# A two-layer hybrid decoder trunk on one core: how densely the adaLN units are strewn among the first mixer's products

## The chip, the core and the metric

The kernel runs on one core of a Trainium2 chip. TensorE (PE in the profile) multiplies matrices, VectorE (DVE), ScalarE (ACT) and GpSimd (POOL) do the rest, and SyncE (SP) starts nearly all DMA transfers from HBM into the on-chip memory. The engines run side by side, each works through its own list of instructions strictly in order, and they wait for one another by semaphores. The metric is the device time of one execution in microseconds, the median over several.

## The reference

A sequence of 256 tokens of width 2048 goes through two layers. Each layer is a token mixer and a SwiGLU block, and each of these four sub-layers is wrapped in a modulation by a condition vector `c` (adaLN) and a layer norm:

```python
def _ada(c, w, b):
    mod = jax.nn.silu(c) @ w + b
    shift, scale, gate = jnp.split(mod, 3, axis=-1)
    return shift[:, None], scale[:, None], gate[:, None]

# one sub-layer
shift, scale, gate = _ada(c, ada_w[layer, s], ada_b[layer, s])
h = x * (1.0 + scale) + shift
y = f(h)                       # a mixer, or SwiGLU
x = _layer_norm(ALPHA * x + (1.0 + gate) * y, ln_g[layer, s], ln_b[layer, s])
```

`c` is one row, so `silu(c) @ w` with `w` of 2048 x 6144 is a matrix times a vector, four times in all. It is little arithmetic on many bytes: 50 MB of f32 weights for each sub-layer.

The first mixer projects `h` with one combined matrix (`proj = h @ w_in`, 2048 x 7472). A part of the columns goes to an mLSTM of eight heads, the other to an RWKV-7 with sixteen heads of 64; the two results are put side by side and multiplied with `w_out`. The second mixer does the same with retention and gated DeltaNet. All is f32.

## The kernel before

**Products.** A product is 256 tokens times a block of 512 columns of a weight matrix. It is made of units of 512 rows of the weight: one unit is one tile of 1 MB (128 x 2048 f32), loaded by SP into one of three buffers called `raw`. ScalarE rounds its two halves to fp32r (`hi`, L703), VectorE subtracts to get the rest (`lo`, L704), and TensorE multiplies (L718, L719, L720: activation high by weight high, high by low, low by high), 24 matmuls of 128 x 512 for a unit. A projection product (`k.product`) has four units.

**adaLN units.** The matrix times vector is done on VectorE. One adaLN unit is 128 of the 6144 outputs of one sub-layer: a tile of 128 x 2048 f32, again 1 MB, is loaded by SP into a buffer of the same three `raw`, multiplied with the broadcast `silu(c)` and summed along its rows in one instruction (L640). A sub-layer has 48 units: 32 for shift and scale, 16 for the gate. There are 192 in all. The first 32 are done before the first mixer, since `h` needs them. The next 48 are strewn among the products of the first mixer: the gate of this mixer (16) and shift and scale of the SwiGLU block behind it (32). The others come in later blocks.

**The rate.** After each unit of a product `fill` adds a rate to a credit and emits as many adaLN units as the credit holds, up to a limit (80 while the first mixer is emitted):

```python
def fill(self, rate):
    ...
    self.ada_credit = getattr(self, "ada_credit", 0.0) + rate
    while self.ada_credit >= 0.999 and self.ada_next < self.ada_limit:
        self.ada(1)
        self.ada_credit -= 1.0
```

**The first mixer** (`mixer_ab`) has twelve such products, 48 units of `w_ab`. Two further blocks of columns and a narrow one have been computed beforehand (`first_products`). RWKV runs in four batches of four heads (`rwkv`): a front (`rwkv_front`, L1163 to L1214), the heads (`rwkv_heads`: small matmuls L1231 and a triangular inverse in `inverses`, whose first part is a chain of shuffles and multiplications on VectorE from L1004 to L1013, then small matmuls L1017 to L1076, then L1249 to L1262) and an output (`rwkv_out`, L1284 to L1307). Products stand between the batches, as the batches need their columns or as work to put aside: one behind the first batch, three behind the second, four behind the third. These are the first eight products. The last four belong to the second half of the mLSTM and are emitted behind the fourth batch (the first half of the mLSTM stands beside that batch). Columns computed early are parked in HBM (`put_by`) and brought back by SP (`fetch`, L1136).

**The order.** What the program emits is not the order in which it runs. At the end of `body` a planner (`Plan`) takes all instructions with their priorities, which go by the place in the program (splits of weights are preferred by some 2000 places), and a cost for each, and lays out for every engine a fixed list by a simulated run. Buffers of one pool are given out in program order: the three `raw` buffers go to weight tiles and adaLN tiles in just the sequence in which the program asks for them, and a buffer is free when the last instruction that reads it is done.

Of the kernel before, what the change touches and what calls it, by code (L numbers as in the profile page):

```python
# [1869 lines left out]
def body(tc, ins, out):  # L1870
    with ExitStack() as stack:
        k = Trunk(tc, ins, out, stack)
        k.setup()
        k.ada_limit = 32
        h, early = k.first_products()
        x = (ins["x"], None)
        k.ada_limit = 80
        side = k.mixer_ab(h, 48.0 / 32, early)
        x, h = k.mix_out(ins["o_ab"], x, 0, side)
        x, h = k.ffn(0, x, h)  # L1880
        k.ada_limit = 176
        k.mixer_cd(h, 32.0 / 44)
        x, h = k.mix_out(ins["o_cd"], x, 2)
        k.ffn(1, x, h)
        plan = Plan(tc, tc.nc, 250)
        plan.prepare(0)
        order, _ = plan.run([x.bass_priority for x in plan.ins])
        plan.impose(order)
# [18 lines left out]
```

## Time and profile before

| | |
|---|---|
| median of three runs | 2782.91 us (2778.63 to 2790.88) |
| the profiled execution | 2782.83 us, span 2780.7 us |
| PE busy | 2639.4 us, 95% of the span |
| DVE busy | 2010.2 us, 72% |
| ACT busy | 1265.2 us, 45% |
| DMA | 681.61 MB, mean 245 GB/s |

The times of the profile count from the start of the span. The products before the first mixer end at about 120 us, the twelve products of the mixer lie between there and about 600 us, its output product and the norm end at about 740 us. An engine's "busy" is the union of its instructions; a wait is the idle time before an instruction, with what released it; PEclk is the share of full clock that TensorE was granted.

### The profile page before, as it was taken

Reading aid. Unit: us, or ns where it says so; the run is one execution under the profiler, and the core shown is the slowest. Engines: PE = TensorE matmul, PEld = TensorE weight load, DVE = VectorE, ACT = ScalarE, POOL = GpSimd, SP = SyncE. Lnnn points to the kernel's source line nnn. Section 1 sums busy time; section 2 is a strip of 40 time slices with the busy share of each in tenths; the row PEclk is TensorE's granted clock in tenths of the full one; section 3 lists DMA queues with packets and bytes.
Section 4 is the critical chain, followed back from the end, with each engine's and each line's share of the span. In section 5 each row is a group of like instructions: output and inputs, shape, how many; then the busy total and the mean of one; then the engine's idle time right before and its main releaser. Section 6 shows DMA issues by size and latency. Waiting matters only on the chain.

```text
span 2780.7 us, 33791 instructions
## 1 busy us (share of the span) xinstructions
PE 2639.4 (95%) x12906; PEld 2157.6 (78%) x12906; DVE 2010.2 (72%) x3153; ACT 1265.2 (45%) x1704; POOL 78.8 (3%) x88
## 2 busy tenths in 40 slices
PE   5598999999999999999999999999999999999997
PEld 3576777788777887788888888878778888888886
DVE  7899877658777567768767898875866646557557
ACT  2364445556634444443446554444454444443442
POOL 0000000110000000000000201100000000000000
PEclk9899999999999999999999999999999999999999
DMA  9988775235578678878866776675657657666554
GB/s 394 364 295 299 261 255 208 91 107 197 199 286 318 226 266 319 317 259 309 324 232 214 257 258 228 250 268 181 232 196 270 244 197 264 220 215 237 199 183 165
DMA packets 109820, 681.61 MB, mean 245 GB/s; under 512 B 12437, under 2 KB 15705, under 8 KB 31577
## 3 DMA queue, kind: packets, MB, share of 16 engines
q1 hardware_dynamic: 108506, 677.36, 67.0%
q8 instruction: 101, 1.65, 0.2%
q10 hardware_dynamic: 1152, 2.10, 0.2%
q14 instruction: 61, 0.50, 0.1%
HBM read 668.89 MB, written 10.52 MB: 244 GB/s over the span
## 4 chain that ended last, share of the span: by engine, by line
PE 63%; DMA 10%; DVE 9%; issue 4%; ACT 3%; POOL 0%; DVEq 0%; ACTq 0%; SPq 0%; POOLq 0%
PE g L720 19%; PE g L719 19%; PE g L718 19%; DMA raw<-ada 3%; DVE lo L704 3%; DMA raw<-gu 3%; DVE raw L640 3%; DMA raw<-w_cd 2%; ACT hi L703 2%; DMA t<-x 1%; PE m L963 1%; DMA t<-lnrow 1%; DMA raw<-w_ab 1%; PE m L1231 0%; PE m L899 0%
## 5 line engine op out<-in xcount | busy, mean ns | idle before, releaser
L704 DVE TENSOR_TENSOR lo<-raw,hi 128x1024 fp32r<-128x1024 f32 (+2 forms) x802 | 971.4, 1217 | 598.5 <-ACT hi L703 594.1
L703 ACT ACTIVATE hi<-raw 128x1024 fp32r<-128x1024 f32 (+2 forms) x802 | 838.1, 1052 | 1143.6 <-PE g L720 855.6
L718 PE MATMUL g<-hi,h 128*128 128x512 f32 (+2 forms) x2312 | 908.4, 394 | 54.8 <-ACT h L782 38.4
L719 PE MATMUL g<-lo,h 128*128 128x512 f32 (+2 forms) x2312 | 909.9, 394 | 10.2 <-DVE lo L704 9.9
L720 PE MATMUL g<-hi,h 128*128 128x512 f32 (+2 forms) x2312 | 906.2, 392 | 0.0
L718 PEld LDWEIGHTS g<-hi,h 128*128 128x128 f32 x2312 | 439.7, 190 | 152.0 <-ACT h L782 41.3
L719 PEld LDWEIGHTS g<-lo,h 128*128 128x128 f32 x2312 | 440.4, 190 | 107.8 <-DVE lo L704 20.6
L720 PEld LDWEIGHTS g<-hi,h 128*128 128x128 f32 x2312 | 440.1, 190 | 86.3 <-issue 1.7
L640 DVE SCALAR_TENSOR_TENSOR raw<-raw,silu_c 128x2048 f32<-128x2048 f32 x176 | 402.6, 2287 | 31.5 <-DMA raw<-ada 22.7
L718 PE MATMUL g<-hi,a 128*128 128x512 f32 x920 | 361.0, 392 | 5.4 <-DVE t L860 5.4
L719 PE MATMUL g<-lo,a 128*128 128x512 f32 x920 | 360.0, 391 | 0.1
L720 PE MATMUL g<-hi,a 128*128 128x512 f32 x920 | 360.0, 391 | 0.0
L718 PEld LDWEIGHTS g<-hi,a 128*128 128x128 f32 x920 | 173.4, 188 | 41.7 <-DVE t L860 5.8
L719 PEld LDWEIGHTS g<-lo,a 128*128 128x128 f32 x920 | 173.5, 189 | 36.4 <-DVE lo L704 0.9
L720 PEld LDWEIGHTS g<-hi,a 128*128 128x128 f32 x920 | 173.4, 189 | 35.7
L1413 DVE SCALAR_TENSOR_TENSOR f<-c,cols_sb,f 128x253 f32<-128x253 f32 (+2 forms) x120 | 56.0, 476 | 4.7 <-ACT f L1410 3.9
L1614 POOL TENSOR_SCALAR s<-cons_sb,log_alpha 128x128 f32<-128x128 f32 x16 | 15.2, 962 | 1017.7 <-DVE log_alpha L1558 882.9
L1084 POOL TENSOR_SCALAR_AFFINE_SELECT a<-a 128x512 f32<-128x512 f32 (+1 forms) x20 | 27.3, 1372 | 323.1 <-ACT a L1233 178.7
L640 DVE SCALAR_TENSOR_TENSOR a<-a,silu_c 128x2048 f32<-128x2048 f32 x16 | 36.3, 2285 | 0.0
L902 ACT ACTIVATE t<-m,affine 128x128 f32<-128x128 f32 x96 | 35.0, 473 | 0.1
L1231 PE MATMUL m<-y 64*128 64x256 f32 x128 | 29.2, 405 | 3.8 <-DVE a L1234 3.7
L966 ACT ACTIVATE a<-m 128x512 fp32r<-128x512 f32 x44 | 26.1, 592 | 13.5 <-PE m L963 12.3
(476 smaller groups left out, 2052.9 us busy)
## 6 DMA issues: line engine op xcount, KB each, us to landing
raw<-ada SPq DMA_DIRECT2D x176, 1024.0 KB, 5.1
raw<-gu SPq DMA_DIRECT2D x176, 1024.0 KB, 4.9
raw<-dn SPq DMA_DIRECT2D x88, 1024.0 KB, 4.8
raw<-w_cd SPq DMA_DIRECT2D x60, 1024.0 KB, 4.8
raw<-w_ab SPq DMA_DIRECT2D x48, 1024.0 KB, 5.1
a<-ada SPq DMA_DIRECT2D x16, 1024.0 KB, 17.0
raw<-o_ab SPq DMA_DIRECT2D x16, 1024.0 KB, 4.8
raw<-o_cd SPq DMA_DIRECT2D x16, 1024.0 KB, 5.4
```

The costliest lines, as they stand in the source:

```text
L640: v.scalar_tensor_tensor(w[:], w[:], 1.0, self.sc[:], ALU.mult, ALU.mult, accum_out=m[:, i:i + 1])
L703: nc.scalar.activation(hi[:, :2 * n], ws, AF.Copy)
L704: nc.vector.tensor_tensor(lo[:, :2 * n], ws, hi[:, :2 * n], ALU.subtract)
L718: mm(o, ah, wh, start=start and k == 0, stop=False)
L719: mm(o, ah, wl, start=False, stop=False)
L720: mm(o, al, wh, start=False, stop=stop and k == 3)
L902: nc.scalar.activation(h32[:, j, :], b[:, P * j:P * j + P], AF.Identity, bias=self.ab[:, sub + 1, 16 + k:17 + k], scale=self.ab[:, sub + 1 ...
L963: nc.tensor.transpose(b[:, P * k:P * k + P], gs[:, t, P * k:P * k + P], self.ident)
L966: nc.scalar.activation(act[:, 0, :, ts], bv, AF.Copy)
L1084: self.nc.gpsimd.affine_select(x, x, pattern=[[0, n] for n in dims] + [[1, P]], compare_op=ALU.is_gt if strict else ALU.is_ge, fill=0.0, b ...
L1231: mm(b[:, T * x:T * x + T], bk[r, c, x, t, :], ar[r, c, t].rearrange("p x s -> p (x s)"), start=True, stop=True)
L1413: v.scalar_tensor_tensor(o[:, d:T], b[:, T * j:T * j + T - d], self.col(wname, 4 * (tile0 + i + j) + 3 - d), o[:, d:T], ALU.mult, ALU.add)
```

## The change

One number in `body`. The rate for the first mixer is 48/48 in place of 48/32: one adaLN unit behind every product unit in place of three behind every two. The 48 adaLN units were all emitted within the first eight products (32 units); now they reach over all twelve (48 units).

```diff
         k.ada_limit = 80
-        side = k.mixer_ab(h, 48.0 / 32, early)
+        side = k.mixer_ab(h, 48.0 / 48, early)
         x, h = k.mix_out(ins["o_ab"], x, 0, side)
```

The number of instructions of each kind stays. Their order moves, and this on all engines, since the planner lays out the lists anew. Three places follow. In the rows the names are those of the program with a running number: `raw` is a buffer of the three, `w_ab` the mixer's weights, `ada` the adaLN weights, `by` a parked block.

SP, at the start of the mixer's first product, before:

```order
L681 DMA raw_1255<-w_ab 128x2048
L681 DMA raw_1289<-ada 128x2048
L681 DMA raw_1292<-ada 128x2048
L1158 DMA q_780<-lw 65x256
L1159 DMA q_780<-la 96x256
L1160 DMA q_780<-lg 128x256
L681 DMA raw_1295<-w_ab 128x2048
L681 DMA raw_1329<-ada 128x2048
L681 DMA raw_1332<-w_ab 128x2048
L681 DMA raw_1366<-ada 128x2048
L681 DMA raw_1369<-ada 128x2048
```

and with the change:

```order
L681 DMA raw_1255<-w_ab 128x2048
L681 DMA raw_1289<-ada 128x2048
L681 DMA raw_1292<-w_ab 128x2048
L1158 DMA q_780<-lw 65x256
L1159 DMA q_780<-la 96x256
L1160 DMA q_780<-lg 128x256
L681 DMA raw_1326<-ada 128x2048
L681 DMA raw_1329<-w_ab 128x2048
L681 DMA raw_1363<-ada 128x2048
L681 DMA raw_1855<-w_ab 128x2048
```

Between two weight tiles stood one adaLN tile and two in turn; now there is one each time.

SP, around the fetch of parked blocks (L1136) that stands between the loads of the tenth and the eleventh product, before:

```order
L681 DMA raw_4569<-w_ab 128x2048
L681 DMA raw_4603<-w_ab 128x2048
L1136 DMA q_3901<-by_3345 128x512 x2
L1136 DMA q_3905<-by_3514 128x4x128 x2
L681 DMA raw_4677<-w_ab 128x2048
L681 DMA raw_4711<-w_ab 128x2048
```

and with the change:

```order
L681 DMA raw_4561<-ada 128x2048
L681 DMA raw_4564<-w_ab 128x2048
L1136 DMA q_3841<-by_3291 128x512 x2
L1136 DMA q_3845<-by_3454 128x4x128 x2
L681 DMA raw_4598<-ada 128x2048
L681 DMA raw_4647<-w_ab 128x2048
L681 DMA raw_4681<-ada 128x2048
L681 DMA raw_4684<-w_ab 128x2048
```

The last sixteen weight tiles had no adaLN tile among them; now each has one.

DVE, in the heads of the third RWKV batch, between the last step of its front and the products with its state (L1255), before:

```order
L1209 TENSOR_TENSOR q_3531<-c_3585,z_3540 128x256
L1061 COPY y_2609<-m_2712 32x8x32
L1061 COPY y_2609<-m_2713 32x8x32
L1185 RECIPROCAL v_3534<-gg_3598 128x1
L1198 SCALAR_TENSOR_TENSOR y_3530<-z_3551,minus_kk,gg_3598 128x2x128
L1186 TENSOR_TENSOR v_3534<-v_3534,gg_3598 128x1
L1199 TENSOR_TENSOR y_3530<-z_3541,gg_3598 128x2x128
L704 TENSOR_TENSOR lo_4538<-raw_4535,hi_4537 128x1024
L1255 TENSOR_TENSOR s_2805<-m_2794,v_2359 128x256
```

and with the change:

```order
L640 SCALAR_TENSOR_TENSOR raw_4411,modulation<-raw_4411,silu_c 128x2048
L1209 TENSOR_TENSOR q_3471<-c_3525,z_3480 128x256
L640 SCALAR_TENSOR_TENSOR raw_4487,modulation<-raw_4487,silu_c 128x2048
L1061 COPY y_2579<-m_2682 32x8x32
L1061 COPY y_2579<-m_2683 32x8x32
L1185 RECIPROCAL v_3474<-gg_3538 128x1
L1198 SCALAR_TENSOR_TENSOR y_3470<-z_3491,minus_kk,gg_3538 128x2x128
L1186 TENSOR_TENSOR v_3474<-v_3474,gg_3538 128x1
L1199 TENSOR_TENSOR y_3470<-z_3481,gg_3538 128x2x128
L704 TENSOR_TENSOR lo_4456<-raw_4453,hi_4455 128x1024
L640 SCALAR_TENSOR_TENSOR raw_4524,modulation<-raw_4524,silu_c 128x2048
L1255 TENSOR_TENSOR s_2775<-m_2764,v_2329 128x256
```

Here no adaLN unit stood; now three do (L640), and a fourth stands right ahead of the second L1255 of this batch.

Counted along DVE's list from one L1004 (the start of a batch's inverse) to the next, the mixer's 48 adaLN units stood 12 ahead of the first batch's, then 19, 15 and 2, and none behind the fourth's. Now they stand 8, 10, 12, 9, and 9 behind the fourth's. The number of weight halves (L704) that precede the fourth batch's L1004 is the same in both lists, 99, and so is the number of product matmuls that precede the third batch's output on PE (L1306), 48.8 units, twelve units of `first_products` among them.

## The prediction

> **What bounds the kernel now.** First the page: who is busy, and whether evenly.
>
> ```profile
> span 2780.7 us, 33791 instructions
> ...
> PE 2639.4 (95%) x12906; PEld 2157.6 (78%) x12906; DVE 2010.2 (72%) x3153; ACT 1265.2 (45%) x1704; POOL 78.8 (3%) x88
> ...
> PE   5598999999999999999999999999999999999997
> ...
> PEclk9899999999999999999999999999999999999999
> DMA  9988775235578678878866776675657657666554
> ```
>
> TensorE sets the pace as a whole. A change that moves work of VectorE and DMA can only give back time in which TensorE waits or runs at a lower clock, or take more of it. So the second view is the busy time by stretches of the first mixer (from about 120 us on).
>
> ```profile
> core 0: us, PE busy (x) PEld busy (x) DVE busy (x) ACT busy (x) POOL busy (x), PEclk, DMA share, GB/s
> ...
> 215.00:260.00 45.00, 35.44 (x140) 26.92 (x139) 40.09 (x86) 13.50 (x15) 0.00 (x0) 0.92 0.90 342
> ...
> 345.00:385.00 40.00, 34.58 (x141) 27.56 (x140) 34.25 (x65) 10.18 (x13) 0.00 (x0) 0.83 0.77 288
> ...
> 470.00:500.00 30.00, 30.00 (x305) 26.15 (x303) 14.62 (x37) 15.46 (x31) 0.00 (x0) 1.00 0.21 72
> 500.00:528.00 28.00, 23.06 (x97) 15.16 (x97) 20.58 (x92) 14.43 (x37) 7.33 (x11) 0.82 0.13 38
> 528.00:600.00 72.00, 71.92 (x530) 62.01 (x529) 45.84 (x132) 38.05 (x65) 4.91 (x10) 1.00 0.34 118
> ```
>
> Two stretches lose: 215 to 260 has 45.00 - 35.44 = 9.56 us of idle PE, and a granted clock of 0.92, which is 0.08 x 35.44 = 2.84 us more; 345 to 385 has 5.42 us idle and 0.17 x 34.58 = 5.88 us of clock. In both VectorE is at 86 to 89% and DMA at 77 to 90%. Beyond 470 us it is the other way round: VectorE and DMA have room, PE is full but for 500 to 528. Third, the waits of PE in 215 to 385, and one of them in order of time:
>
> ```profile
> PE g L718 <- ACT hi L703: 10.7, 6, 3.0
> PE g L719 <- DVE lo L704: 3.2, 6, 0.5
> PE m L1017 <- DVE y L1013: 1.2, 2, 1.0
> ```
>
> ```profile
> 218.55 0.39 PE L720 MATMUL g<-hi,h 128*128 128x512 f32 x1
> 221.72 0.73 PE L718 MATMUL g<-hi,h 128*128 128x512 f32 x2 [2.79 <-ACT hi L703]
> 222.98 0.79 PE L719 MATMUL g<-lo,h 128*128 128x512 f32 x1 [0.53 <-DVE lo L704]
> 223.57 0.63 PE L720 MATMUL g<-hi,h 128*128 128x512 f32 x1
> 224.00 0.63 PE L718 MATMUL g<-hi,h 128*128 128x512 f32 x1
> ...
> 226.81 0.39 PE L718 MATMUL g<-hi,h 128*128 128x512 f32 x1
> 227.04 0.40 PE L719 MATMUL g<-lo,h 128*128 128x512 f32 x1
> ```
>
> Nearly all the waiting is for weights that haven't been split (10.7 + 3.2 us), and behind such a wait matmuls follow at 0.43 us in place of 0.23 for some 3 us: the clock loss belongs to the same stalls. Why the weights are late stands in SP's list:
>
> ```profile
> 213.29 0.33 SPq L681 DMA_DIRECT2D raw<-w_ab  x1
> 216.13 0.33 SPq L681 DMA_DIRECT2D raw<-ada  x1
> 220.13 0.33 SPq L681 DMA_DIRECT2D raw<-w_ab  x1
> 224.19 2.65 SPq L681 DMA_DIRECT2D raw<-ada  x2
> 230.58 0.33 SPq L681 DMA_DIRECT2D raw<-w_ab  x1
> ...
> 261.40 0.33 SPq L681 DMA_DIRECT2D raw<-w_ab  x1
> ```
>
> From 213.29 to 261.40 six weight tiles and nine adaLN tiles pass through the three buffers, 8.02 us for a unit of product. TensorE needs 24 x 0.2275 = 5.46 us for one (0.2275 is the step between matmuls from 226.81 on).
>
> **The change, part by part.** *The supply.* A product unit brings 2 tiles through the buffers in place of 2.5. If a tile keeps its time, a unit comes every 8.02 x 2/2.5 = 6.41 us. The shortfall against 5.46 goes from 2.56 to 0.95 us, so 63% of the loss goes. If the weights that were split ahead, or other work of PE, fill the rest, all goes. The loss is 9.56 + 2.84 + 5.42 + 5.88 = 23.7, less 1.2 us for the wait on L1013, which isn't one for weights: 22.5 us. So 14.2 to 22.5 us come back. Where between them, I take from VectorE's list:
>
> ```profile
> L640 DVE SCALAR_TENSOR_TENSOR raw<-raw,silu_c 128x2048 f32<-128x2048 f32 x50 | 114.2, 2284 | 4.1 <-DMA raw<-ada 4.0
> L704 DVE TENSOR_TENSOR lo<-raw,hi 128x1024 fp32r<-128x1024 f32 x72 | 89.4, 1246 | 32.0 <-ACT hi L703 31.7
> ```
>
> An adaLN unit is 2.284 us of VectorE. Up to the start of the fourth batch's inverse the new list has 39 of them in place of 48 and the same number of halves to split; PE has the same product units behind it when the third batch puts out its result. Nine units fewer are 9 x 2.284 = 20.6 us. VectorE does not pace all of that time, but this lies within the bounds and near the end at which PE is kept full. I take 20.6.
>
> The starts of the four inverses show the same from the side of the batches:
>
> ```profile
> 206.75 0.29 DVE L1004 TENSOR_TENSOR e<-s 128x128 f32<-128x128 f32 x1
> ...
> 322.30 0.28 DVE L1004 TENSOR_TENSOR e<-s 128x128 f32<-128x128 f32 x1
> ...
> 438.34 0.28 DVE L1004 TENSOR_TENSOR e<-s 128x128 f32<-128x128 f32 x1
> ...
> 517.74 0.28 DVE L1004 TENSOR_TENSOR e<-s 128x128 f32<-128x128 f32 x1
> ```
>
> 115.6 us with 19 adaLN units between two starts, 116.0 with 15, and 79.4 with 2.
>
> *Units that come to stand in the third batch's heads.* Four now lie on VectorE between that batch's front and its second L1255, where there was none. There its list is a chain with PE:
>
> ```profile
> 479.38 0.42 DVE L1209 TENSOR_TENSOR q<-c,z 128x256 f32<-128x256 f32 x1 [0.38 <-PE c L1208]
> 482.08 0.88 DVE L1061 COPY y<-m 32x256 f32<-32x256 f32 x2 [2.27 <-PE m L1058]
> ...
> 490.02 1.23 DVE L704 TENSOR_TENSOR lo<-raw,hi 128x1024 fp32r<-128x1024 f32 x1 [5.44 <-ACT hi L703]
> 492.34 0.42 DVE L1255 TENSOR_TENSOR s<-m,v 128x256 f32<-128x256 f32 x1 [1.10 <-PE m L1253]
> ```
>
> Behind the new units wait L1061 and L1255, and behind these the matmuls L1069 and L1261. VectorE sat idle there for 2.27 and 5.44 us, so a unit may fit in free of cost, or an instruction comes while it runs. Bounds: 0 and 4 x 2.284 = 9.1 us. I take half a unit each, 4.6 us, since no row tells at which moment of the wait the unit starts.
>
> *Nine units behind the fourth batch's L1004.* 20.6 us of VectorE and 9 MB of transfers move to where VectorE is busy 45.84 of 72 us, DMA 34% and PE 71.92 of 72: the product matmuls of PE hide them, so 0. If this cover were gone, up to 9 x 2.284 = 20.6 us.
>
> *SP.* Nine issues of 0.33 us move past the fetch of parked blocks, at which the queue stands for long:
>
> ```profile
> SPq L1136 <- PE c L1306: 43.9, 1, 43.9
> ```
>
> The fetch waits for a tile that the third batch's output frees, and this does not change; behind it now stand an adaLN tile and then the weights of the eleventh product, one tile (some 3.2 us, from 48.1 us for 15 tiles) later. PE has products left at that time: 0.
>
> *Elsewhere.* The planner lays out the second mixer a little differently too, with the same instructions. PE is idle for 22.5 us there in all:
>
> ```profile
> sum 700.00, PE 677.52 PEld 562.24 DVE 550.22 ACT 343.19 POOL 41.19; mean PE 24.20 PEld 20.08 DVE 19.65 ACT 12.26 POOL 1.47
> ```
>
> (1400 to 2100 us.) No row says which way this goes: 0, with some 5 us to either side.
>
> **The sum**, against the profiled execution (2782.83 us, 2.1 us more than its span, and within 0.1 us of the median): 2782.83 - 20.6 + 4.6 = 2766.8, say **2767 us**. Own range with the bounds: 2782.83 - 22.5 = 2760 to 2782.83 - 14.2 + 9.1 = 2778.
>
> **The rivals.** *Only traded (2778 us).* The stalls go by the low rule (14.2 us) and the four units in the third batch's heads cost their full 9.1 us: 2782.83 - 14.2 + 9.1 = 2777.7. For it: that batch is where PE is least covered (23.06 of 28 us, clock 0.82) and the batches' spacing above was shortest where the list had only 2 units. Against: at 470 to 500, where the four lie, PE is busy 30.00 of 30.
>
> *The clock does not come back (2775 us).* Behind the second stretch PE ran slowly while it was busy:
>
> ```profile
> 372.00:378.00 6.00, 5.67 (x26) 5.61 (x27) 3.84 (x9) 2.00 (x3) 0.00 (x0) 0.57 0.58 210
> ```
>
> If that goes with the small matmuls of the heads, and not with the stalls, only the idle time returns: 14.98 - 1.2 = 13.8 us, of it 20.6/22.5, 12.6 us; 2782.83 - 12.6 + 4.6 = 2774.8. [...]
>
> *All comes back (2760 us).* 22.5 us, and the four units fit into the idle time of VectorE: 2782.83 - 22.5 = 2760.3.
>
> *Slower (2798 us).* The units land where the batches are chains: all four in the third batch's heads and the nine behind the fourth's start cost their full length, 13 x 2.284 = 29.7 us, against 14.2 us: 2782.83 + 15.5 = 2798.3. It decides from the point where more than six of the thirteen (14.2 / 2.284) are waited for in full. For it: L1061, L1255 and their like in the fourth batch queue right behind units. Against: 71.92 of 72 us of PE at 528 to 600.
>
> **How the numbers follow.** The forecast has a chance of 0.48, only traded 0.20, clock 0.10, all 0.12, slower 0.10. A measurement here tells about 0.5%, 13.9 us, from no change: below 2769.0 is faster, above 2796.8 slower. The forecast lies just beyond the first bound, 0.6 of its chance is faster (0.29), with all 0.12 and 0.05 from the spread of the others: 0.46. Slower: 0.09 of the last. The same: 0.45. For 8 in 10 the range leaves out most of the last rival and reaches past "all" by the 5 us of the second mixer and some noise: 2752 to 2789.
>
> **What would show it.** In the changed kernel's profile, the waits of PE for L703 and L704 between 200 and 385 us should fall from 13.9 to under 4 us, with a clock of 0.97 or more there; the first, second and third gaps between the starts L1004 should be about 95, 109 and 95 us (each by its number of units: -9, -3, +7), the fourth start 20 us or more earlier; PE stays full from there to 600 us. It is wrong if weights still come late at two tiles for a unit, if waits for L1061 or L1255 by several us appear in the third batch, or if PE falls below 95% busy in the 80 us behind the fourth start.

## The result

The changed kernel takes 2769.61 us in the median of 10 runs (2756.61 to 2783.07), the kernel before 2785.36 us in 10 runs beside it (2776.68 to 2790.88): a ratio of 0.9939, 95% interval 0.9918 to 0.996. In a second set it took 2766.66 us (11 runs, 2757.38 to 2786.43) against 2783.28 (20 runs): 0.9934, 0.9912 to 0.9956. So it is faster by 16 us, 0.6%, and the forecast of 2767 us is met. Single runs of either kernel lie further apart than this (the changed one's by 26 to 29 us in a set, those of the kernel before by 14 to 35), so only medians and means over many runs can show it.

### The profile page after: what moved, and what is told of

It is laid out like the page before. It is cut to its first block, busy times and chain, and to the rows that moved or that the text cites. A ratio compares the mean times of both kernels' runs of the same rounds, so it can differ in the third digit from the quotient of the medians.

```text
span 2762.5 us, 33778 instructions
## 1 busy us (share of the span) xinstructions
PE 2633.9 (95%) x12906; PEld 2155.9 (78%) x12906; DVE 2007.0 (73%) x3153; ACT 1263.0 (46%) x1702; POOL 78.7 (3%) x88
## 4 chain that ended last, share of the span: by engine, by line
PE 67%; DMA 15%; DVE 12%; ACT 3%; issue 2%; POOL 0%; SPq 0%; DVEq 0%; ACTq 0%; POOLq 0%
PE g L720 20%; PE g L719 20%; PE g L718 20%; DMA raw<-ada 5%; DMA raw<-gu 4%; DVE lo L704 4%; DVE raw L640 4%; DMA a<-ada 2%; ACT hi L703 2%; DMA raw<-w_cd 1%; PE m L963 1%; DMA raw<-w_ab 1%; DMA y<-w_ab 1%; DMA t<-x 1%; PE m L1231 1%
## 5 line engine op out<-in xcount | busy, mean ns | idle before, releaser
L704 DVE TENSOR_TENSOR lo<-raw,hi 128x1024 fp32r<-128x1024 f32 (+2 forms) x802 | 968.4, 1214 | 581.9 <-ACT hi L703 579.1
L703 ACT ACTIVATE hi<-raw 128x1024 fp32r<-128x1024 f32 (+2 forms) x802 | 837.7, 1052 | 1132.2 <-PE g L720 877.4
L719 PE MATMUL g<-lo,h 128*128 128x512 f32 (+2 forms) x2312 | 909.6, 393 | 10.7 <-DVE lo L704 10.5
L640 DVE SCALAR_TENSOR_TENSOR raw<-raw,silu_c 128x2048 f32<-128x2048 f32 x176 | 402.7, 2288 | 43.7 <-DMA raw<-ada 35.5
L640 DVE SCALAR_TENSOR_TENSOR a<-a,silu_c 128x2048 f32<-128x2048 f32 x16 | 36.3, 2285 | 0.0
L963 PE MATMUL m<-cons_sb,q 128*128 128x128 f32 x176 | 28.4, 285 | 6.1 <-DVE q L960 6.1
L963 PEld LDWEIGHTS m<-cons_sb,q 128*128 128x128 f32 x176 | 21.0, 144 | 13.4 <-DVE q L960 12.0
```

What stands on the lines that cost most here:

```text
L640: v.scalar_tensor_tensor(w[:], w[:], 1.0, self.sc[:], ALU.mult, ALU.mult, accum_out=m[:, i:i + 1])
L703: nc.scalar.activation(hi[:, :2 * n], ws, AF.Copy)
L704: nc.vector.tensor_tensor(lo[:, :2 * n], ws, hi[:, :2 * n], ALU.subtract)
L719: mm(o, ah, wl, start=False, stop=False)
L963: nc.tensor.transpose(b[:, P * k:P * k + P], gs[:, t, P * k:P * k + P], self.ident)
```

## The profile after

The page of the changed kernel, in the order of the prediction:

```profile
span 2762.5 us, 33778 instructions
...
PE 2633.9 (95%) x12906; PEld 2155.9 (78%) x12906; DVE 2007.0 (73%) x3153; ACT 1263.0 (46%) x1702; POOL 78.7 (3%) x88
...
PE   5699999999999999999999999999999999999997
...
PEclk8799999999999999999999999999999999999999
DMA  9966765546588578778866775665657657666554
```

The shares of the whole have hardly moved; the difference is seen only by stretches. The busy time in the stretches that the prediction looked at (times from the start of the span; the batches now start 14 to 29 us earlier, so the last three rows hold other work than before):

```profile
200.00:385.00 185.00, 181.51 (x1161) 145.92 (x1161) 153.37 (x359) 92.34 (x168) 5.78 (x8) 1.00 0.67 247
215.00:260.00 45.00, 43.66 (x337) 35.70 (x337) 39.49 (x74) 21.32 (x33) 0.00 (x0) 1.00 0.82 301
345.00:385.00 40.00, 38.16 (x328) 30.08 (x326) 28.91 (x74) 21.50 (x51) 2.00 (x2) 1.00 0.56 206
470.00:500.00 30.00, 25.18 (x110) 17.39 (x109) 22.94 (x97) 16.91 (x38) 7.36 (x11) 0.89 0.22 71
500.00:528.00 28.00, 28.00 (x153) 24.03 (x152) 27.05 (x59) 15.73 (x25) 0.00 (x0) 1.00 0.69 244
528.00:600.00 72.00, 68.66 (x480) 57.04 (x480) 55.26 (x140) 37.91 (x70) 11.28 (x15) 0.95 0.55 200
```

The same first row of the kernel before:

```profile
200.00:385.00 185.00, 166.31 (x884) 129.89 (x883) 163.05 (x344) 79.46 (x133) 8.63 (x10) 0.94 0.77 280
```

From 200 to 385 us PE is idle for 185 - 181.51 = 3.5 us, where it was idle for 18.7; its clock is 1.00 in place of 0.94, and VectorE does 9.7 us less. The waits of PE in this stretch, all that are left:

```profile
PE m L1231 <- DVE a L1234: 1.0, 3, 0.7
PE g L719 <- DVE lo L704: 0.7, 2, 0.4
PE m L1069 <- ACT y L1062: 0.6, 1, 0.6
PE m L1069 <- DVE y L1061: 0.5, 1, 0.5
PE c L1179 <- DVE z L1094: 0.5, 1, 0.5
```

The wait for `hi` (10.7 us before) is gone and that for `lo` went from 3.2 to 0.7. SP's list shows the tiles in turn, one and one:

```profile
215.56 0.33 SPq L681 DMA_DIRECT2D raw<-ada  x1
218.17 0.33 SPq L681 DMA_DIRECT2D raw<-w_ab  x1
...
251.28 0.33 SPq L681 DMA_DIRECT2D raw<-ada  x1
252.42 0.33 SPq L681 DMA_DIRECT2D raw<-w_ab  x1
258.45 0.33 SPq L681 DMA_DIRECT2D raw<-ada  x1
```

Six product units in 258.45 - 215.56 = 42.89 us, 7.15 us each, where six took 48.11. The step worked out from the tiles alone was 6.41 us. The buffers are not what it waits for now: no weight is late by more than 0.4 us. The four inverses start at

```profile
192.69 0.29 DVE L1004 TENSOR_TENSOR e<-s 128x128 f32<-128x128 f32 x1
288.81 0.28 DVE L1004 TENSOR_TENSOR e<-s 128x128 f32<-128x128 f32 x1
392.31 0.28 DVE L1004 TENSOR_TENSOR e<-s 128x128 f32<-128x128 f32 x1
488.38 0.28 DVE L1004 TENSOR_TENSOR e<-s 128x128 f32<-128x128 f32 x1
```

96.1, 103.5 and 96.1 us apart, against 115.6, 116.0 and 79.4.

## The experiments

The table gives each run that follows: time and ratio to the kernel before, the fourth start of L1004, the issue of the first gate row (L673, behind the fourth batch), and the waits of PE for split weights (`hi` and `lo`) from 120 to 600 us. The last three are of one profiled execution each, which need not be near the median. Line numbers shift by a few where a kernel has lines added.

| kernel | median us | ratio (95%) | fourth start | gate row | waits for weights |
|---|---|---|---|---|---|
| before | 2785.36 | | 517.74 | 637.21 | 14.5 |
| before, again | 2780.81, one run | | 515.79 | 636.06 | 13.3 |
| changed | 2769.61 | 0.9939 (0.9918 to 0.996) | 488.38 | 610.64 | 0.7 |
| changed, again | 2766.66 | 0.9934 (0.9912 to 0.9956) | 503.82 | 626.12 | 0.5 |
| sums cut short | 2770.87 | 0.9949 (0.9931 to 0.9967) | 507.80 | 628.35 | 12.9 |
| loads cut short | 2766.26 | 0.994 (0.9916 to 0.9964) | 500.57 | 620.99 | 9.1 |
| third gap's sums cut | 2762.93 | 0.9919 (0.9892 to 0.9946) | 483.22 | 605.33 | 0.5 |
| last nine sums cut | 2765.39 | 0.993 (0.9902 to 0.9958) | 497.66 | 617.82 | 2.3 |
| six units with five | 2776.79 | 0.9977 (0.995 to 1.0005) | 508.67 | 628.69 | 7.0 |
| eight units with nine | 2783.18 | 0.9986 (0.9956 to 1.0017) | 487.57 | 629.68 | 3.3 |
| changed, extra matmuls | 2770.13 | 0.9928 (0.9897 to 0.996) | 492.40 | 625.19 | 4.7 |
| before, extra matmuls | 2774.96 | 0.9965 (0.9936 to 0.9994) | 502.81 | 627.57 | 18.6 |

Every run, profiled or not, has its span and its mean granted clock. So span x (1 - clock) is counted as what the clock took from it, and the rest of the span as work and idle time. The means over the runs, with those of the kernel before that ran beside them (for the first row its 41 runs of two sets; standard errors: 0.8 to 3.1 us for the clock, 0.7 to 2.6 for the rest):

| kernel | taken by the clock | before | rest of the span | before |
|---|---|---|---|---|
| changed, 21 runs | 57.1 | 59.5 | 2709.1 | 2722.9 |
| sums cut short | 50.9 | 58.9 | 2717.3 | 2723.4 |
| loads cut short | 47.5 | 60.0 | 2717.9 | 2722.4 |
| third gap's sums cut | 54.9 | 60.0 | 2704.9 | 2722.4 |
| last nine sums cut | 53.9 | 60.0 | 2709.7 | 2722.4 |
| six units with five | 64.4 | 60.0 | 2711.6 | 2722.4 |
| eight units with nine | 64.0 | 61.8 | 2717.8 | 2724.6 |
| changed, extra matmuls | 52.4 | 61.8 | 2715.5 | 2724.6 |
| before, extra matmuls | 52.5 | 61.8 | 2723.9 | 2724.6 |

### Both kernels a second time

No edit. What was expected of the kernel before:

> The kernel before once more, for a second execution in profile. The two profiles so far differ by 25.6 us up to the norm behind the first mixer (722.6 and 697.0 us), but the block behind it, in which both programs hold the same instructions in the same order, took 748.4 us in the one and 758.8 in the other. If these 10 us are the spread of executions, this one's SwiGLU block lies anywhere from 745 to 760 us while its fourth inverse start lies within 3 us of 517.7. If they belong to the changed kernel, it lies within 3 us of 748.

and of the changed one:

> The changed kernel once more. Fourth inverse start within 3 us of 488.4, norm within 4 us of 697. If the 10 us in the SwiGLU block are the spread of executions, that block takes anything from 745 to 760 us and the ratio stays near 0.994 only because both kernels' later parts vary; if the changed kernel causes them, it takes 756 to 761 us again.

The two profiles of the kernel before are alike: all four starts within 2 us (206.61, 321.10, 437.31, 515.79), the waits for weights 9.8 + 3.5 us. Those of the changed kernel are not. (This is no property of the new order alone: over 20 to 29 runs the kernel before scatters by 24 to 35 us.) Its waits for weights are gone again (0.5 us), but its starts are 193.76, 297.60, 407.93 and 503.82, 15 us later at the fourth than in the first profile, with the same instructions in the same order. In 200 to 385 us PE is as busy as in the first profile, at a lower clock:

```profile
200.00:385.00 185.00, 181.49 (x1088) 147.52 (x1086) 143.89 (x318) 87.08 (x149) 3.79 (x6) 0.92 0.65 238
```

The head of a batch shows where it is lost. The second execution, from just before the first L1069 (254.02 us) on:

```profile
250.00:254.00 4.00, 4.00 (x109) 2.82 (x107) 3.94 (x6) 3.85 (x6) 0.00 (x0) 1.00 0.42 133
254.00:258.00 4.00, 3.39 (x37) 2.98 (x36) 1.35 (x2) 2.87 (x9) 0.00 (x0) 0.86 0.96 393
258.00:262.00 4.00, 4.00 (x21) 4.00 (x20) 1.28 (x2) 0.53 (x2) 0.00 (x0) 0.50 0.63 221
262.00:266.00 4.00, 4.00 (x14) 3.42 (x15) 2.11 (x7) 1.06 (x1) 0.00 (x0) 0.50 0.33 139
...
270.00:274.00 4.00, 4.00 (x17) 3.63 (x16) 0.48 (x3) 1.24 (x4) 0.00 (x0) 0.50 0.73 254
274.00:278.00 4.00, 4.00 (x30) 3.44 (x30) 0.43 (x1) 1.29 (x4) 0.10 (x1) 1.00 0.02 8
```

and the first execution (L1069 at 253.12 us):

```profile
254.00:258.00 4.00, 3.61 (x40) 3.40 (x40) 1.88 (x1) 2.50 (x8) 0.00 (x0) 1.00 0.97 401
258.00:262.00 4.00, 4.00 (x31) 3.75 (x31) 2.86 (x9) 1.06 (x1) 0.00 (x0) 1.00 0.65 219
262.00:266.00 4.00, 4.00 (x33) 3.66 (x33) 4.00 (x7) 1.23 (x4) 0.00 (x0) 1.00 0.14 59
```

For some 16 us the clock is 0.50 in the one and 1.00 in the other, with PE busy 4.00 us in each row from 258 to 274 us in the one and 3.82 to 4.00 in the other. This one dip made the first gap 103.8 in place of 96.1 us (a gap is the time from one start of L1004 to the next). What PE does as the clock falls:

```profile
254.02 0.67 PE L1069 MATMUL m<-y,a 64*64 64x64 f32 x8
255.30 0.68 PE L1069 MATMUL m<-y,a 64*64 64x64 f32 x8 [0.61 <-ACT y L1062]
255.91 0.43 PE L1249 MATMUL m<-q,a 128*128 128x64 f32 x2
256.27 1.46 PE L1076 MATMUL m<-y,P 64*64 64x64 f32 x16
257.66 1.54 PE L1249 MATMUL m<-q,a 128*128 128x64 f32 x6
```

64-wide matmuls, one wait of 0.61 us, and no product until 262.38 us. Counted over the heads of the first three batches, the clock fell to 0.50 right behind L1069 in 7 of 12 heads of the four profiles with the changed order (the first two, and the two below with sums cut in it), and in none of 12 of the four profiles with the order of before. In these one or several product matmuls stand between the groups in most heads, though one head of before has 5.8 us without any and kept its clock both times. The order of before has its half-clock stretches in other places: from 120 us to the gate row the clock took 20.5 us in both its profiles, 15.4 and 29.0 in the two of the changed kernel.

The SwiGLU block behind the mixer (from the first DMA of L920 at the end of one norm to that of the next) took 748.5 and 753.0 us in the kernel before, 758.9 and 758.8 in the changed one. So a part of the first difference is the spread of executions, and the 6 to 10 us that are left come with the changed kernel.

### The sums of the adaLN units cut short

In the kernel before, order unchanged; the 48 units of the mixer are summed over 256 of their 2048 columns:

```diff
+        n = 256 if 32 <= u < 80 else D
-        v.scalar_tensor_tensor(w[:], w[:], 1.0, self.sc[:], ALU.mult, ALU.mult, accum_out=m[:, i:i + 1])
+        v.scalar_tensor_tensor(w[:, :n], w[:, :n], 1.0, self.sc[:, :n], ALU.mult, ALU.mult, accum_out=m[:, i:i + 1])
```

> Rate 48/32 as before and the order of the kernel before on every engine, all 48 adaLN tiles loaded in full, but the sum of the mixer's 48 units runs over 256 of 2048 columns (7/8 of these sums are left out), so about 0.5 us of VectorE in place of 2.28. If VectorE's time makes the weights late (the term of 20.6 us: so many units, so much VectorE), the waits of PE for the split weights fall from 14.5 to under 4 us, the fourth inverse start comes at 490 us or earlier and the whole time falls by 20 us or more. If the loads through the three buffers do (15 tiles in 48 us, DMA at 90%), at least half of the waits stay, the start lies at 503 us or later and the time falls by under 12 us.

A sum falls from 2.284 us to 0.416:

```profile
L641 DVE SCALAR_TENSOR_TENSOR raw<-raw,silu_c 128x256 f32<-128x256 f32 x48 | 20.0, 416 | 8.8 <-DMA raw<-ada 8.8
```

This takes 48 x 1.87 = 90 us from VectorE, and the fourth start comes 8 to 10 us earlier, the time falls by 12 to 14 us: 8.0 us of it by the clock and 6.1 by the rest. The waits for weights stay at 12.9 us:

```profile
PE g L719 <- ACT hi L704: 8.5, 6, 4.0
PE g L720 <- DVE lo L705: 4.4, 8, 0.8
```

So VectorE's time is a part of what the adaLN units cost, but by itself not what makes the weights late.

### The loads of the adaLN units cut short

In the kernel before, order unchanged; each of the 48 tiles loads 256 of its columns, and VectorE works on seven times these:

```diff
+        elif 32 <= u < 80:
+            w = self.raw_p.tile([P, 2048], F32, tag="raw", name=self.name("raw"))
+            nc.sync.dma_start(w[:, :256], src[:, :256])
...
+            seven = lambda x: x.rearrange("p (r n) -> p r n", r=7)
+            v.scalar_tensor_tensor(seven(w[:, 256:]), w[:, :256].unsqueeze(1).to_broadcast([P, 7, 256]), 1.0, seven(self.sc[:, 256:]), ALU.mult, ALU.mult, accum_out=m[:, i:i + 1])
```

> The kernel before, its order unchanged on every engine; each of the first mixer's 48 adaLN tiles loads only 256 of its 2048 columns, while VectorE's sum keeps nearly its length (seven times the same 256 columns, 1792 in place of 2048). Theory 'loads': the weights are late because nine adaLN tiles of 1 MB pass through the three buffers beside six weight tiles. Then the waits of PE for L703 and L704 in the mixer fall from 14.5 us to under 4, the fourth L1004 starts at 495 us or earlier (before: 517.7 and 515.8), and the time falls by 18 us or more. Theory 'VectorE': the sums hold up the splits. Then the waits stay at 11 us or more, the fourth start at 512 or later, and the time within 8 us of before. With the shortened sums having given about half of the gain, a share of both would show as a fourth start between these.

Between the two: the fourth start at 500.57 us, 16 us earlier, the time 17 us less, the waits for weights 9.1 us in place of 14:

```profile
PE g L727 <- ACT hi L712: 5.1, 5, 1.8
PE g L728 <- DVE lo L713: 4.0, 8, 0.7
```

The sums still take 2.01 us each. The loads are the larger part of the lateness (5 of 14 us of the waits, against 1 us for the sums), and neither alone ends it. Most of the 17 us, though, came by the clock, which took 12.5 us less; the rest of the span fell by 4.5 us, no more than with the sums cut (6.1). Why the clock gained is not shown. The account that fits both: a tile holds its buffer for the load and for the sum, so either keeps the next weight out, and taking the whole unit away, as the change does nine times up to the fourth start, removes both. This is argued, not shown. Load and sum were not cut in one kernel, so it stays open whether a tile's place in the sequence of the three buffers costs something even when both are short. Both theories were too simple.

### Six units with every five

```diff
-        side = k.mixer_ab(h, 48.0 / 32, early)
+        side = k.mixer_ab(h, 48.0 / 40, early)
```

> Five... six adaLN units with every five product units in place of three with every two (48.0 / 40): a middle way. Units up to the four L1004: 41, 54, 66, 78, against 44, 63, 78, 80 before and 40, 50, 62, 71 in the changed kernel. If the supply of weights sets the gain, the first two gaps (13 and 12 units against 19 and 15) get most of it already: waits for L703 and L704 under 5 us and a fourth start of 495 to 508 us, the time 6 to 14 us below before. If only the full step down to one unit matters, waits stay at 9 us or more and the time within 5 us of before.

Waits 7.0 us, half of before; fourth start 508.67; 6.4 us faster, with an interval that reaches just past 1. The waits lie between the two bounds that were set, and the start just misses its own. Beside the clock the gain is 10.8 us, of the 13.8 of the whole change; the clock took 4.4 us more, about twice the error of this difference. So what the units cost beside the clock falls as they are taken out of the early gaps, and the clock hides a part of it.

### The sums of the third gap cut short

In the changed kernel, order unchanged:

```diff
+        n = 256 if 62 <= u < 71 else D
```

with the line of the sums as above.

> The changed kernel, its order unchanged; the nine adaLN units between the third and the fourth L1004 are summed over 256 columns in place of 2048, some 18 us less of VectorE there. If the adaLN units cost what the forecast's sum gives them (2.284 us each of the path), the third gap falls from 96 us to about 80 and the time by some 16 us. If instead TensorE's own products fill that gap now (two product units more than in the kernel before stand in it), the gap stays within 4 us of 96 and the time within 6 us of the changed kernel.

The third gap is 483.22 - 393.65 = 89.6 us, against 96.1 and 95.9: 6.4 us less for 9 x 1.87 = 16.8 us of VectorE. But the clock differs too. The gap here, and in the first profile of the changed kernel:

```profile
393.65:483.22 89.57, 86.88 (x565) 69.21 (x563) 57.44 (x188) 46.44 (x87) 3.69 (x5) 1.00 0.64 231
392.31:488.38 96.07, 91.94 (x565) 72.91 (x563) 73.62 (x189) 46.68 (x87) 3.68 (x5) 0.95 0.59 216
```

The same 565 matmuls keep PE busy for 86.88 us at full clock and for 91.94 at 0.95. The idle time falls only from 4.1 us (5.5 in the second profile) to 2.7: 1.4 to 2.8 us for the 16.8, so a unit costs some 0.1 to 0.2 of its length in this gap. What made the gap grow from 79.4 to 96 us is PE's own work: 565 matmuls where there were 512, 2.2 product units more (2.2 x 5.46 = 12.0 us), and the lower clock. The prediction's "about 95, by its number of units" gave the right size from a rule that does not hold.

### The last nine sums cut short

```diff
+        n = 256 if 71 <= u < 80 else D
```

> The changed kernel, its order unchanged; the last nine adaLN units, behind the fourth L1004, are summed over 256 columns in place of 2048, some 18 us less of VectorE there. The prediction's step: the products of TensorE hide them, they cost 0. Then the stretch from the fourth L1004 to the fetch of the first gate row (L673) stays at 120 us or more (122.3 us in both profiles of the changed kernel, 119.5 in that of the kernel before), and the time within 5 us. If they cost their length (the rival 'slower'), the stretch falls to about 104 us. If part of the cover is missing, to 115 or so.

From the fourth start to the gate row: 617.82 - 497.66 = 120.2 us, against 122.3 in both profiles of the changed kernel. Taking 16.8 us of the nine sums away gains 2 us at most; TensorE hides the rest. The time is within 5 us of the changed kernel.

### Eight units with every nine, the rest behind the gate row

The change carried on, to see where that cover ends:

```diff
-        side = k.mixer_ab(h, 48.0 / 48, early)
+        side = k.mixer_ab(h, 48.0 / 54, early)
...
         self.gate = self.gate_rows(self.a8, sub)
+        if sub == 0:
+            self.ada(max(0, 80 - self.ada_next))
```

> The change carried on: eight adaLN units with every nine product units (48.0 / 54), and the rest, behind the first gate row, at once. Units up to the four L1004: 38, 48, 56, 64 in place of 40, 50, 62, 71, so 16 in place of 9 behind the fourth. By the third gap's experiment (89.6 us with nine sums cut short, 96 with nine full ones) the third gap falls by 0 to 5 us; by that of the last nine (2 us at most) the seven more behind the fourth start cost 0 to 4 us, or 16 us if the cover of TensorE is used up by the nine. So the time is 2 us shorter to 5 us longer than the changed kernel; 10 us longer would say that the cover ended.

The cover ended, which was not expected. The fourth start is at 487.57 us, no earlier than the best of the changed kernel, and from there to the gate row it takes 142.1 us in place of 122.3. This stretch, and the same of the changed kernel:

```profile
487.57:629.68 142.11, 126.97 (x758) 102.42 (x757) 121.31 (x284) 70.75 (x120) 22.11 (x24) 0.95 0.65 237
488.38:610.64 122.26, 116.80 (x715) 96.75 (x716) 101.75 (x263) 72.19 (x121) 17.43 (x24) 0.94 0.56 198
```

Of the 20 us, 9.7 are idle time of PE (15.1 in place of 5.5 us) for seven units more (16.0 us of VectorE); the other 10.2 are 43 matmuls more, work that stood ahead of the fourth start. By the ratios the time is 14 us above that of the changed kernel. Set against the kernel before, each in its own set, 7.0 us of the gain beside the clock are gone, and the clock took 2.2 us more where the changed kernel has 2.4 less. The waits of PE from the fourth start to the gate row:

```profile
PE g L718 <- ACT hi L703: 6.3, 2, 5.3
PE g L719 <- DVE lo L704: 2.6, 2, 2.3
PE c L1305 <- DVE s L1307: 2.0, 2, 1.4
```

and the place, behind the product rows, where the output's weights are late:

```profile
600.00:630.00 30.00, 21.08 (x87) 15.10 (x87) 27.80 (x49) 17.97 (x35) 10.86 (x7) 0.77 0.76 283
```

The wait for `hi` is back, 9 us idle over this row and a clock of 0.77: the same stall as before the change, in another place.

### Extra matmuls in the heads

Is it the stretch without a product that brings the clock down? In the changed kernel, eight matmuls of 128x512 for each of the first three batches, written ahead into banks that the small matmuls then overwrite:

```diff
+    def warm(self, x):
+        for _ in range(2 if self.hot is not None else 0):
+            self.nc.tensor.matmul(x[:], self.hot[:, 0, 0, 0:P], self.hot[:, 0, 0:2, :].rearrange("p k t -> p (k t)"), start=True, stop=True)
...
             x = self.bank()
+            self.warm(x)
             for j in range(4):
                 mm(x[64:, 64 * j:64 * j + 64], mt[:64, hs.start + j, 64:], d[:64, hs.start + j, :64], start=True, stop=True)
...
             xb = self.bank()
+            self.warm(xb)
```

> The changed kernel with 24 matmuls more in the first mixer's heads: ahead of the first writes into four of the small matmuls' banks of each of the first three batches, two matmuls of 128x512 whose result is overwritten (8 x 0.23 = 1.8 us for a batch, 5.5 us in all). Nearly all else keeps its order. In the changed kernel the granted clock fell to 0.50 for 7 to 12 us behind the first L1069 in 7 of 12 heads seen so far, where some 5 us of 64-wide matmuls stand without a product between them. Theory 'gaps between products': the dips come from these stretches. Then no head, or one of three, shows the dip; the clock loss of a run (span x (1 - granted clock), 57.1 us in the mean over 21 runs of the changed kernel) falls by 6 us or more, and the times scatter less than 29 us; the time comes out within 5 us of the changed kernel, since 5.5 us are paid. Theory 'chance': the dips do not depend on what PE does there. Then some half of the heads show it, the clock loss stays at 55 us or more, and the time is some 5 us longer.

and the same in the kernel before:

> The same 24 matmuls in the kernel before, where none of 12 heads seen in this order had the dip. It measures what they cost by themselves: some 5 us slower than before if PE is full there, 0 if they fall into its waits; the clock loss of a run stays near the 59.5 us of the 41 runs of before. If that falls by 6 us too, the extra matmuls act on something else than the heads' dips.

In the changed kernel with the extra matmuls the clock takes 52.4 us in the mean of 12 runs (standard error 3.1), against 57.1 (1.5) in 21 runs without; the rest of the span grows by 6.4 us (2709.1 to 2715.5), about the 5.5 us that the matmuls need. The fall of 4.7 us lies between what the two theories asked for, and its own error is 3.4 us. Of the profile's three heads one has the dip, a long one. The time came out even, and the runs scatter no less (2745.18 to 2789.84). So this run does not decide between the theories.

In the kernel before the loss falls as well, from 61.8 us (standard error 1.9, 29 runs of the same set) to 52.5 (2.8, 10 runs), with no dip in any head in either, and the rest of the span stays (2724.6 and 2723.9): the time falls by 10 us, and all of it is clock. In the profile two half-clock stretches that both profiles of before have, 10.24 us each in 369 to 383 and in 516 to 527 us, are missing. So more went than dips behind L1069. But the extra matmuls are not the only thing that moved: the plan was laid out anew, 46.5 product units in place of 48.8 precede the fourth start on PE, and the waits for weights rose to 18.6 us. So these runs show that the clock's loss can fall by some 10 us from one kernel to another (61.8 to 52.5 us here; 60.0 to 47.5 with the loads cut short, where the order is that of the kernel before); that the extra matmuls themselves hold the clock up they do not show.

## Why the prediction was right, and where it was not

**The supply (-20.6 us).** The mechanism holds. The waits for L703 and L704 fell from 13.9 to 0.7 us (forecast: under 4). The fourth start came 29 us earlier in one profile and 13 in the other, 19 with the last nine sums cut (which can't matter before it): 20 in the mean, with the clock's share in it. From 120 us to that start PE runs the same 2118 matmuls in both orders and is idle for 29.9 and 28.4 us before, 12.2 and 16.1 after: 12 to 18 us less, where the term had 12.6 us of idle time. The size of 20.6 us came from a price that does not hold, VectorE's 9 x 2.284 us, after a section that laid the lateness to the buffers. The two cuts show load and sum both at work, and the third gap shows a unit at 0.1 to 0.2 of its length where weights aren't late. That it is the stalls that make a unit dear fits this, but no run shows it by itself.

**What of it was clock.** Of the 22.5 us, 8.7 were clock, laid to the stalls. (The rows give somewhat more, 0.08 x 45.00 + 0.17 x 40.00 = 10.4 us: the clock is a mean over the whole stretch, so it goes with its length and not with PE's busy time.) The clock of those stretches did come back in the first profile: 1.00 in 215 to 260 and in 345 to 385. In the second it was 0.92 from 200 to 385, where the forecast asked for 0.97. Over the runs, the clock's share is 57.1 us (21 runs of the changed kernel) against 59.5 (41 runs of the kernel before): 2.4 us came back, within the error of 1.9. The step that failed is "the clock loss belongs to the same stalls". Half of it never did: its longest piece,

```profile
372.86:383.10 10.24, 10.24 (x46) 9.66 (x46) 8.08 (x15) 1.73 (x3) 0.00 (x0) 0.50 0.43 146
```

costs 5.1 us in the second batch's heads with PE full, and in the second profile of the same kernel it begins at 369.24 us, behind a wait of 1.72 us for L1013 and ahead of the next late weight. And the changed order has dips of its own in the heads. "The clock does not come back" was right in that little of it did (the 2.4 us above); that the loss goes with the small matmuls of the heads, no run shows by itself. Its price of 2775 us was too high: it had 12.6 us of idle time come back and 4.6 us paid, 8.0 us net, and the spans without the clock's share differ by 2722.9 - 2709.1 = 13.8 us.

**The third batch's heads (+4.6).** Too much, within its bounds. PE's waits for L1061 from 120 to 600 us are 1.6 us in all, against 0.5:

```profile
PE m L1069 <- DVE y L1061: 1.6, 2, 1.0
```

The same place paid in clock instead, in the first profile:

```profile
450.00:460.00 10.00, 10.00 (x42) 8.26 (x40) 2.73 (x3) 4.34 (x7) 0.00 (x0) 0.52 0.36 125
```

VectorE is busy 2.73 of the 10 us there, so the units are not what it waits for.

**Nine units behind the fourth start (0).** 2 us at most, as shown by cutting them. In the 80 us behind the start PE is busy 77.37 (97%) and 77.67 us in the two profiles, against 78.21 before. The rival "slower" had its mechanism right as well: it needed more than this change puts there. With seven units more the stall comes back, and the kernel is no faster than before within what can be measured (0.9986, up to 1.0017).

**The gaps** of 95, 109 and 95 us are 96.1, 103.5 and 96.1 in one profile, 103.8, 110.3 and 95.9 in the other, where the first two hold a dip each.

**Elsewhere (0, with 5 to either side).** From the gate row to the end of the span took 2143.5 and 2142.6 us before, 2151.9 and 2158.6 after. Some 6 us of this are work of PE that now stands behind the gate row (busy time x clock, summed over windows of 5 us: from 150 us to the gate row 443.9 and 444.4 us before, 435.2 and 434.0 after; from there to the second gate row 536.2 and 535.6 before, 539.6 and 539.8 after; from the second to the third 723.5 and 723.7 before, 725.7 and 726.5 after). The remaining 2 to 10 us have no one place in the profiles, and their cause stays open; PE is idle for 51 and 49 us behind the gate row in the kernel before and for 55 and 57 in the changed one.

**The sum.** 2767 us was met by 2769.61 and 2766.66, but not by its terms. Split by the shares of the 22.5 us, the forecast's 16 us were 12.6 of idle time and 8.0 of clock, less 4.6; the runs show 13.8 us beside the clock, where it had 8.0 net, and 2.4 of clock, where it had 8.0. Two errors of some 6 us stood against each other, so it was luck that the sum came out. Neither "only traded" nor "all comes back" is what the profiles show.

## What to carry to other kernels

Spread the side loads that share buffers with the main stream until the main one is never late, and no further: 1.5 units for a product left 14 us of stalls, 1.0 under 1 us, and 0.89 with the rest at the end brought the same stall back behind the last batch, with half of the gain beside the clock and nearly all of the time lost. Before laying a loss to one resource, cut the load and the work of the suspected unit apart: here each alone left most of the waits in place. And count idle time and clock apart, in forecasts and in experiments: cutting the loads looked like 17 us and was 4.5 beside the clock, and an order with less idle time on TensorE (12.2 and 16.1 us in place of 29.9 and 28.4) left the clock's share where it was within the error (57.1 us against 59.5).

## What was not expected of the hardware

The granted clock stood at 0.50 for many microseconds with PE busy 4.00 of 4.00 us, in some executions of a program and not in others: from 258 to 274 us in the second profile of the changed kernel, where the first, with the same instructions in the same order, has 1.00. This dip cost 7.7 us. The dips of these profiles reach from stretches of a few microseconds (below) to 27 us (439 to 467 us in the changed kernel with extra matmuls, where PE was busy 4.25 to 5.00 of each 5 us). The first profile of the changed kernel has three dips from 150 us to the gate row, the second five, and the clock took 13.7 of the 15.4 us by which its fourth start lies later. Over the 21 runs the span goes with the clock's share at a correlation of 0.92 (slope 1.08), and what is left of the span scatters by only 3.2 us (standard deviation).

From 150 us to the gate row the stretches at 0.50 last 3.41 us (four of them) and 10.24 us (two) in the first profile of the kernel before, 10.24, 6.83 and 6.83 us in that of the changed one. A dip in the second profile of the changed kernel, with the 3.41 us ahead of it:

```profile
465.13:468.54 3.41, 3.41 (x36) 2.99 (x36) 0.82 (x1) 1.69 (x6) 0.00 (x0) 1.00 0.59 247
468.54:475.37 6.83, 6.83 (x23) 5.39 (x22) 2.72 (x3) 3.51 (x5) 0.00 (x0) 0.50 0.44 154
```

PE was recorded busy throughout both rows, so idle time of PE did not come right ahead of this dip. What starts a dip, and why one execution has it and another does not, no run shows.
